# Long rows, a later sum of squares, half-K products and an early split in a two-layer decoder trunk

## The chip, the core and the metric

The kernel runs on one core of a Trainium2 chip. The core has five engines that run their own instruction streams in order: TensorE (PE for its matmuls, PEld for its weight loads), VectorE (DVE), ScalarE (ACT), GpSimd (POOL) and SyncE (SP, which here only issues DMAs). The metric is the time of one execution on the device in microseconds, the median over several runs.

## The reference

The program computes two layers of a decoder over 256 tokens plus 16 learned meta tokens put in front (272 columns in all), with a model width of 2048.

```
layer 0:  h += gla(rmsnorm(h))            # gated linear attention, 4 heads
          h += relu(rmsnorm(h) W_up)^2 W_down          # width 8192
shared:   k, v = rmsnorm(h) W_kv ; rotary on k
layer 1:  h += swa(rmsnorm(h) W_q, k, v)  # window 128, sinks, 32 query and 4 key heads
          h += relu(rmsnorm(h) W_up)^2 W_down
out = rmsnorm(h), the meta tokens dropped
```

The end of the linear attention is what the change touches most. Per head of 512 value columns:

```
o = o * rsqrt(mean(o*o) + eps) * norm_out
o = o * silu(gate)            # gate is part of xn @ w_in
h = h + o @ w_out
```

Everything is float32, and the result has to hold to nearly that precision.

## The kernel before, in words

Activations lie transposed: 128 channels of the model on the partitions, tokens along the free dimension. `h` is 16 such tiles (KT = 16) of 272 tokens. TensorE multiplies in the faster float32r format, so every operand is split in two: a high part, which is the value rounded by a cast, and a low part, the value less the high part. A product is made of three passes per k (128 rows of K): high by high, high by low, low by high.

**Weights.** `fetch` (line 79) brings half a weight tile, 128x1024 float32, by a DMA that SP issues. `split_weight` (line 86) makes its high part on ACT (line 89) and its low part on DVE (line 91); three buffers hold each. `product` (line 122) makes one output tile of 128 columns: 8 k with the first half of the weights, 8 k with the second, all into one PSUM bank of the pool `acc`, which has four. For 256 tokens `passes` (line 105) joins the two passes of the high weights in one matmul of 512 columns (lines 114 and 115), else it issues three (lines 118 to 120).

**Activations.** The class `Split` (line 98) holds both parts of an activation tile. In memory the order is (a, s, j): token 2j + a, part s, so a tile is four rows: even high, even low, odd high, odd low. The views `hi`, `lo` and `both` that the matmuls read walk through tokens in order, so they alternate between an even row and an odd row. Five places make such splits, each with one instruction on ACT for the high part and one on DVE for the low part: `split_x` (lines 161 and 162) for the inputs of each projection, the gate stage (lines 700 and 701), the MLP's hidden tiles (lines 730 and 731), and attention's output `O` (lines 899 and 900, and 932 and 933). Their producers write through the same views.

**Gate stage** (lines 668 to 702). For each head g, `mix(g)` makes four output tiles on TensorE (lines 674 to 676), copies them to `OT` on ACT, squares them on ACT and adds the squares on POOL. `so.rstd` then splits the sum (lines 188 and 189), adds over partitions by two matmuls with ones (lines 190 and 191), and derives the reciprocal root by ACT and DVE (lines 197 to 204). Four multiplications scale `OT` (line 681). After that come the head's four gate tiles: a product with 16 k (line 688), a scaling (690), a clamp on POOL (692), three ACT functions (693 to 695), two multiplications on DVE (696 and 697), and the split to `y`.

**First output projection.** `residual` (line 146) makes the 16 output tiles one after the other, each over all 16 `y`, adds each to `h` (line 151) and calls `finish`, which splits the new `h` for the MLP and adds up its squares.

**Shared K/V and layer 1's queries** (lines 788 to 806). Four K/V products run side by side in four banks, first all four with the first half of K, then all with the second. During the second half, the query inputs `xq` are split from `h`. Sixteen buffers of the tag `x` serve both the K/V input `xk` and `xq`, so an `xq` tile waits until the `xk` tile whose slot it takes has been multiplied. Eight of them are split in the loop, two after each product of the second half; the other eight follow behind the loop. A rotary step (`rope`, lines 766 to 776) on K stands between them: its DMAs go through POOL's queue and DVE waits for them at line 775.

**Order.** A planner puts the instructions in order: it simulates the engines with a cost model and takes, for each engine, what is ready, by the order of the source. In the attention stage TensorE's order is written out by hand (line 942), ACT's and DVE's is the planner's. On the chip every engine runs its list in order, and an instruction that waits holds up all behind it on that engine. `tc.issue_after(ins)` adds an edge of order only: what the block issues on the engine of `ins` comes behind `ins`; the other engines are left alone.

Of the kernel before, what the change touches and what calls it, by code (L numbers as in the profile page):

```python
# [19 lines left out]
P = 128  # L20
D = 2048
KT = D // P
HK = KT // 2
NM = 16
SEQ = 256
# [39 lines left out]
def trunk(ctx: ExitStack, tc: tile.TileContext, a: dict, out: bass.AP):  # L65
# [28 lines left out]
    def pairs_of(t):  # L94

        return t.rearrange("p (j a) -> p j a", a=2)

    class Split:


        def __init__(self, tile_, n):
            self.n, self.both = n, tile_[:, :2 * n].rearrange("p (a s j) -> p s j a", a=2, s=2)
            self.hi, self.lo = self.both[:, 0], self.both[:, 1]

    def passes(ps, hi, lo, xs, first, last, m=P, apart=True):
# [3 lines left out]
        for k, x in enumerate(xs):  # L109
            wh, wl = hi[:, k * m:(k + 1) * m], lo[:, k * m:(k + 1) * m]  # L110
            begin, end = first and k == 0, last and k == len(xs) - 1
            if wide:
                both = ps[:, :2 * n].rearrange("p (s j a) -> p s j a", s=2, a=2)
                nc.tensor.matmul(both, wh, x.both, start=begin, stop=False)  # L114
                nc.tensor.matmul(both[:, 1], wl, x.hi, start=False, stop=end)  # L115
            else:
                out = pairs_of(ps[:, :n])
                nc.tensor.matmul(out, wh, x.hi, start=begin, stop=False)  # L118
                nc.tensor.matmul(out, wh, x.lo, start=False, stop=False)  # L119
                nc.tensor.matmul(out, wl, x.hi, start=False, stop=end)  # L120

# [23 lines left out]

    def residual(src_w, ys, cols, finish, rounds=1, between=None):

        for r in range(rounds):
            for m in range(KT):
                for term in product(src_w[m], ys, halves=(0, 1) if rounds == 1 else (r,), apart=between is None or r > 0):  # L150
# [6 lines left out]

    def split_x(src, scale_col):
        x = Split(xp.tile([P, 2 * L], F32R, tag="x", name="x"), src.shape[-1])
        src = pairs_of(src)  # L160
        nc.scalar.activation(x.hi, src, AF.Copy, scale=scale_col)
        nc.vector.scalar_tensor_tensor(x.lo, src, scale_col, x.hi.bitcast(F32), ALU.mult, ALU.subtract)  # L162
        return x
# [59 lines left out]
    with ExitStack() as gla:  # L223
# [444 lines left out]
        def mix(g):  # L668
            so = Square()
            OT[g] = yp.tile([P, 4, L], F32, tag="OT", bufs=2, name="OT")  # L670
            for m in range(4):
# [6 lines left out]
                so.add(OT[g][:, m], square=nc.scalar.square)  # L678
            ro = so.rstd(512, "rso", bufs=2, split=True)
            for m in range(4):  # L680
                nc.vector.tensor_mul(OT[g][:, m], OT[g][:, m], ro)

        ys = []
        for m in range(KT):
            g, mm = divmod(m, 4)
            if mm == 0:
                mix(g)
            ps, = product(a["w_in"][32 + m], xs)
# [6 lines left out]
            nc.scalar.activation(sg, sg, AF.Exp, scale=-1.0)  # L695
            nc.vector.tensor_mul(gt, gt, sg)
            nc.vector.scalar_tensor_tensor(gt, OT[g][:, mm], no[:, mm:mm + 1], gt, ALU.mult, ALU.mult)
            y = Split(yp.tile([P, 2 * L], F32R, tag="y", bufs=KT, name="y"), L)
            gt = pairs_of(gt)
            nc.scalar.copy(y.hi, gt)  # L700
            nc.vector.tensor_sub(y.lo, gt, y.hi.bitcast(F32))
            ys.append(y)

        xs, sq = [], Square()
# [6 lines left out]

        residual(a["w_out_a"], ys, slice(0, L), next_norm(1))

    def mlp(layer, xs, sq, cols, finish):
        n = cols.stop - cols.start
        rs = sq.rstd(D, "rs", split=True)
        with tc.tile_pool(name="hid", bufs=KT) as hp, tc.tile_pool(name="wp2", bufs=1) as wp2:
            for b in range(NB):
                hs = []
                for m in range(KT):  # L720
# [7 lines left out]
                    y = Split(hp.tile([P, 2 * L], F32R, tag="hid", name="hid"), n)  # L728
                    u2 = pairs_of(u2)
                    nc.scalar.copy(y.hi, u2)  # L730
                    nc.vector.tensor_sub(y.lo, u2, y.hi.bitcast(F32))
                    hs.append(y)
# [19 lines left out]
    with ExitStack() as swa:  # L752
# [11 lines left out]
        m1, m2, m3 = ld("m1", [P, P]), ld("m2", [P, SEQ]), ld("m3", [P, L])  # L764

        def rope(dst, src, cols):

# [20 lines left out]
        kv = [acc.tile([P, 512], F32, tag="acc", name="ps") for _ in range(4)]  # L788
        xq, vts = [], []
        for i in range(2):  # L790
            for m in range(4):
                hi, lo = split_weight(fetch(a["w_kv"][m][i]))
                passes(kv[m], hi, lo, xk[i * HK:(i + 1) * HK], i == 0, i == 1)
                if i == 0:
                    continue
                xq += [split_x(h[k][:, X], qgains[:, k:k + 1]) for k in range(2 * m, 2 * m + 2)]
# [20 lines left out]

        O = ap.tile([P, KT, 2, 2, SEQ // 2], F32R, name="O")

        def attended(part, ms, tokens):  # L820

            return O[:, ms, :, part, tokens.start // 2:tokens.stop // 2].rearrange("p m a j -> p m j a")
        N1, N3 = P - NM, NM
# [26 lines left out]
        class Step:  # L850
# [39 lines left out]
            def values(self):  # L890
# [6 lines left out]
                oh, ol = (attended(part, slice(m0, m0 + 2), slice(0, N2)) for part in range(2))  # L897
                pv = pv.rearrange("p i (j a) -> p i j a", a=2)
                nc.scalar.copy(oh, pv)
# [24 lines left out]
            def last_values(self):  # L924
# [4 lines left out]
                ms = slice(self.pair * GRP, (self.pair + 1) * GRP)  # L929
                src = ps[:, :P].rearrange("p (i j a) -> p i j a", i=GRP, a=2)  # L930
                oh, ol = (attended(part, ms, slice(N2, SEQ)) for part in range(2))
# [142 lines left out]
```

## Time and profile before

| | |
|---|---|
| median of 3 runs | 2062.76 us (2061.18 to 2065.05) |
| the profiled execution | 2060.31 us |
| its span, first to last instruction | 2058.6 us |
| mean granted TensorE clock | 0.997 |
| PE busy, PEld busy | 2030.5 us, 1951.3 us |
| DVE, ACT, POOL busy | 1404.8, 1130.7, 202.3 us |
| read from HBM | 376.82 MB, 184 GB/s over the span |

Times in the profile count from the first instruction. `L91` is line 91 of the kernel. A group's row has the engine, the operation, the tiles written and read, the number of instructions, and durations in nanoseconds as least, median and greatest, or the sum of busy time and a mean. A row of waits has who waited for whom, the total in microseconds, how often, and the longest. Matmuls are pipelined and their ends are modelled, so the distance between two starts says more than a duration.

### The profile page before, as it was taken

To read this page: it belongs to the slowest core of one execution; us is meant where nothing else is said; L and a number is where in the kernel's file an instruction comes from. 1 tells how busy PE (TensorE), PEld (TensorE's weight loads), DVE (VectorE), ACT (ScalarE), POOL (GpSimd) and SP (SyncE) were. 2 spreads that over 40 slices of the span, in tenths; PEclk is the share of its full clock that TensorE was granted. 3 is DMA by queue.
4 is the path that set the end of the run, shared out by engine and by line. 5 is a ranking of instruction groups with operands and counts; after the bars stand their busy time and mean duration, and the time that the engine had idled before them with its cause. 6 is when DMAs were issued, how large, how long until landed. Compare 5 with 4: busy or idle time off the path is not lost. (4 is left out here: it accounts for less than half of the span.)

```text
span 2058.6 us, 39099 instructions
## 1 busy us (share of the span) xinstructions
PE 2030.5 (99%) x15978; PEld 1951.3 (95%) x15978; DVE 1404.8 (68%) x1999; ACT 1130.7 (55%) x1729; POOL 202.3 (10%) x209
## 2 busy tenths in 40 slices
PE   9999999999999999999999999999999999999997
PEld 9999999999999999999999988999999999999997
DVE  7799677766556556655667777697666666666776
ACT  7565665455345435534554578756546545644653
POOL 0000233300000000000024111060000000000032
PEclk9999999999999999999999999999999999999999
DMA  7644445565655555555554654466666666666662
GB/s 242 194 160 142 150 144 180 189 230 190 192 188 191 189 192 187 192 188 193 186 190 154 203 161 141 135 229 211 203 199 203 200 201 202 201 200 203 200 200 103
DMA packets 109124, 383.85 MB, mean 186 GB/s; under 512 B 13328, under 2 KB 15888, under 8 KB 108944
## 3 DMA queue, kind: packets, MB, share of 16 engines
q1 hardware_dynamic: 106640, 378.29, 56.9%
q0 software_dynamic: 1152, 2.38, 0.4%
q8 instruction: 125, 2.05, 0.4%
q10 hardware_dynamic: 1152, 0.68, 0.1%
q14 instruction: 55, 0.45, 0.1%
HBM read 376.82 MB, written 2.10 MB: 184 GB/s over the span
## 5 line engine op out<-in xcount | busy, mean ns | idle before, releaser
L91 DVE TENSOR_TENSOR lo<-raw,hi 128x1024 fp32r<-128x1024 f32 x707 | 872.4, 1235 | 468.8 <-ACT hi L89 460.8
L89 ACT CAST hi<-raw 128x1024 fp32r<-128x1024 f32 x707 | 740.4, 1048 | 782.4 <-PE ps L119 435.8
L119 PE MATMUL ps<-x,hi 128*128 128x272 f32 (+1 forms) x2032 | 567.4, 279 | 2.3 <-DVE x L162 2.3
L118 PE MATMUL ps<-x,hi 128*128 128x272 f32 (+1 forms) x2032 | 568.6, 280 | 0.0
L120 PE MATMUL ps<-x,lo 128*128 128x272 f32 (+1 forms) x2032 | 567.6, 280 | 0.3 <-DVE lo L91 0.3
L119 PEld LDWEIGHTS ps<-x,hi 128*128 128x128 f32 x2032 | 385.5, 190 | 2.9 <-DVE x L162 2.7
L118 PEld LDWEIGHTS ps<-x,hi 128*128 128x128 f32 x2032 | 385.5, 190 | 2.6 <-issue 2.1
L120 PEld LDWEIGHTS ps<-x,lo 128*128 128x128 f32 x2032 | 385.3, 190 | 1.1 <-DVE lo L91 0.6
L114 PE MATMUL ps<-x,hi 128*128 128x512 f32 x1024 | 335.9, 382 | 0.0
L114 PE MATMUL ps<-hid,hi 128*128 128x512 f32 x1008 | 330.1, 382 | 0.0
L118 PE MATMUL ps<-hid,hi 128*128 128x272 f32 (+1 forms) x1040 | 290.1, 279 | 0.0
L119 PE MATMUL ps<-hid,hi 128*128 128x272 f32 (+1 forms) x1040 | 290.1, 279 | 0.0
L120 PE MATMUL ps<-hid,lo 128*128 128x272 f32 (+1 forms) x1040 | 290.1, 279 | 0.0
L115 PE MATMUL ps<-x,lo 128*128 128x256 f32 x1024 | 279.2, 273 | 0.0
L115 PE MATMUL ps<-hid,lo 128*128 128x256 f32 x1008 | 274.1, 273 | 0.0
L114 PEld LDWEIGHTS ps<-x,hi 128*128 128x128 f32 x1024 | 193.5, 189 | 27.0 <-DVE x L162 0.2
L114 PEld LDWEIGHTS ps<-hid,hi 128*128 128x128 f32 x1008 | 190.2, 189 | 26.4
L115 PEld LDWEIGHTS ps<-x,lo 128*128 128x128 f32 x1024 | 196.6, 192 | 0.3 <-DVE lo L91 0.3
L118 PEld LDWEIGHTS ps<-hid,hi 128*128 128x128 f32 x1040 | 196.6, 189 | 0.0
L119 PEld LDWEIGHTS ps<-hid,hi 128*128 128x128 f32 x1040 | 196.6, 189 | 0.0
L120 PEld LDWEIGHTS ps<-hid,lo 128*128 128x128 f32 x1040 | 196.6, 189 | 0.0
L115 PEld LDWEIGHTS ps<-hid,lo 128*128 128x128 f32 x1008 | 193.5, 192 | 0.2
(259 smaller groups left out, 2214.0 us busy)
## 6 DMA issues: line engine op xcount, KB each, us to landing
raw<-in_w_up SPq DMA_DIRECT2D x256, 512.0 KB, 4.2
raw<-in_w_down SPq DMA_DIRECT2D x256, 512.0 KB, 4.2
raw<-in_w_in SPq DMA_DIRECT2D x91, 512.0 KB, 3.4
raw<-in_w_out_a SPq DMA_DIRECT2D x32, 512.0 KB, 4.0
raw<-in_w_q SPq DMA_DIRECT2D x32, 512.0 KB, 3.6
raw<-in_w_out_b SPq DMA_DIRECT2D x32, 512.0 KB, 3.4
raw<-in_w_kv SPq DMA_DIRECT2D x8, 512.0 KB, 3.5
sw<-qt POOLq DMA_DIRECT2D x32, 64.0 KB, 4.3
```

What stands on the lines that cost most here:

```text
L89: nc.scalar.copy(hi, raw)
L91: nc.vector.tensor_sub(lo, raw, hi.bitcast(F32))
L114: nc.tensor.matmul(both, wh, x.both, start=begin, stop=False)
L115: nc.tensor.matmul(both[:, 1], wl, x.hi, start=False, stop=end)
L118: nc.tensor.matmul(out, wh, x.hi, start=begin, stop=False)
L119: nc.tensor.matmul(out, wh, x.lo, start=False, stop=False)
L120: nc.tensor.matmul(out, wl, x.hi, start=False, stop=end)
```

## The change

Four edits.

1. *Rows.* `Split` gets two more views, `hi_runs` and `lo_runs`, that walk through all even tokens and then all odd ones. The producers (the five places above) write through them and read their source at a step of two tokens. What lies in memory, and what the matmuls read, is as before. For `O` the same is done in `attended` and in the views of its PSUM source.
2. *Squares.* `mix` no longer ends with the sum. A new `mixed(g, so)` holds it, with its matmuls ordered behind the newest gate matmul (`newest[0]`). The loop over heads makes `mix`, the first two gate products with their activation functions (`gate_product`), then `mixed`, then the gating and split of these two tiles (`gated`), and then the other two tiles whole.
3. *Halves of K.* `residual` gets `begin`; the first output projection passes 3. The first three output tiles run side by side in three banks: first half of K for all three, then the second half.
4. *Early split.* `split_x` can write into a given place. Eight of the query inputs (k from 8 to 15) are split during the first half of the K/V products, into the tiles of `O`, which attention fills only later; `O` is declared earlier for it.

```diff
+    def runs_of(t):
+        return t.rearrange("p (j a) -> p a j", a=2)
 class Split:
+            runs = tile_[:, :2 * n].rearrange("p (a s j) -> p s a j", a=2, s=2)
+            self.hi_runs, self.lo_runs = runs[:, 0], runs[:, 1]
+    newest = [None]
 def passes(...)
-                nc.tensor.matmul(out, wl, x.hi, start=False, stop=end)
+                newest[0] = nc.tensor.matmul(out, wl, x.hi, start=False, stop=end)
-    def residual(src_w, ys, cols, finish, rounds=1, between=None):
+    def residual(src_w, ys, cols, finish, rounds=1, between=None, begin=0):
+            if begin:
+                banks = [acc.tile([P, 512], F32, tag="acc", name="ps") for _ in range(begin)]
+                for i in range(2):
+                    for m, ps in enumerate(banks):
+                        hi, lo = split_weight(fetch(src_w[m][i]))
+                        passes(ps, hi, lo, ys[i * HK:(i + 1) * HK], i == 0, i == 1)
+                        if i == 1:
+                            nc.vector.tensor_add(h[m][:, cols], h[m][:, cols], ps[:, :ys[0].n])
+                            finish(m)
-            for m in range(KT):
+            for m in range(begin, KT):
-    def split_x(src, scale_col):
-        x = Split(xp.tile([P, 2 * L], F32R, tag="x", name="x"), src.shape[-1])
-        src = pairs_of(src)
-        nc.scalar.activation(x.hi, src, AF.Copy, scale=scale_col)
-        nc.vector.scalar_tensor_tensor(x.lo, src, scale_col, x.hi.bitcast(F32), ALU.mult, ALU.subtract)
+    def split_x(src, scale_col, room=None):
+        x = Split(xp.tile([P, 2 * L], F32R, tag="x", name="x") if room is None else room, src.shape[-1])
+        src = runs_of(src)
+        nc.scalar.activation(x.hi_runs, src, AF.Copy, scale=scale_col)
+        nc.vector.scalar_tensor_tensor(x.lo_runs, src, scale_col, x.hi_runs.bitcast(F32), ALU.mult, ALU.subtract)
...
-            ro = so.rstd(512, "rso", bufs=2, split=True)
+            return so
+        def mixed(g, so):
+            with tc.issue_after(newest[0].ins):
+                ro = so.rstd(512, "rso", bufs=2, split=True)
             for m in range(4):
                 nc.vector.tensor_mul(OT[g][:, m], OT[g][:, m], ro)
...
+        for g in range(GH):
+            so = mix(g)
+            waiting = [gate_product(4 * g + m) for m in range(2)]
+            mixed(g, so)
+            for m, gt in enumerate(waiting):
+                gated(4 * g + m, gt)
+            for m in range(2, 4):
+                gated(4 * g + m, gate_product(4 * g + m))
-        residual(a["w_out_a"], ys, slice(0, L), next_norm(1))
+        residual(a["w_out_a"], ys, slice(0, L), next_norm(1), begin=3)
...
                 if i == 0:
+                    late_xq += [split_x(h[k][:, X], qgains[:, k:k + 1], O[:, k].rearrange("p a s j -> p (a s j)")) for k in range(HK + 2 * m, HK + 2 * m + 2)]
                     continue
...
-        xq += [split_x(h[k][:, X], qgains[:, k:k + 1]) for k in range(HK, KT)]
+        xq += late_xq
```

The splits of the gate stage, the MLP and attention change in the same way as `split_x`: `runs_of` in place of `pairs_of` for the source, and the `_runs` views for the target.

More of the change, by code (lines that the diff above doesn't have):

```diff
@@ L114, in passes @@
                 nc.tensor.matmul(both, wh, x.both, start=begin, stop=False)
-                nc.tensor.matmul(both[:, 1], wl, x.hi, start=False, stop=end)
+                newest[0] = nc.tensor.matmul(both[:, 1], wl, x.hi, start=False, stop=end)
             else:
@@ L683, in trunk, with gate_product @@
         ys = []
[L684 to L687, printed above, removed]
+        def gate_product(m):
             ps, = product(a["w_in"][32 + m], xs)
@@ L696, in trunk, with gated @@
             nc.vector.tensor_mul(gt, gt, sg)
+            return gt
+        def gated(m, gt):
+            g, mm = divmod(m, 4)
             nc.vector.scalar_tensor_tensor(gt, OT[g][:, mm], no[:, mm:mm + 1], gt, ALU.mult, ALU.mult)
             y = Split(yp.tile([P, 2 * L], F32R, tag="y", bufs=KT, name="y"), L)
-            gt = pairs_of(gt)
-            nc.scalar.copy(y.hi, gt)
-            nc.vector.tensor_sub(y.lo, gt, y.hi.bitcast(F32))
+            gt = runs_of(gt)
+            nc.scalar.copy(y.hi_runs, gt)
+            nc.vector.tensor_sub(y.lo_runs, gt, y.hi_runs.bitcast(F32))
             ys.append(y)
+        for g in range(GH):
[6 more added lines that the diff above has]
+                gated(4 * g + m, gate_product(4 * g + m))
         xs, sq = [], Square()
@@ L728, in mlp @@
                     y = Split(hp.tile([P, 2 * L], F32R, tag="hid", name="hid"), n)
-                    u2 = pairs_of(u2)
-                    nc.scalar.copy(y.hi, u2)
-                    nc.vector.tensor_sub(y.lo, u2, y.hi.bitcast(F32))
+                    u2 = runs_of(u2)
+                    nc.scalar.copy(y.hi_runs, u2)
+                    nc.vector.tensor_sub(y.lo_runs, u2, y.hi_runs.bitcast(F32))
                     hs.append(y)
@@ L764, in trunk @@
         m1, m2, m3 = ld("m1", [P, P]), ld("m2", [P, SEQ]), ld("m3", [P, L])
+        O = ap.tile([P, KT, 2, 2, SEQ // 2], F32R, name="O")
         def rope(dst, src, cols):
@@ L788, in trunk @@
         kv = [acc.tile([P, 512], F32, tag="acc", name="ps") for _ in range(4)]
-        xq, vts = [], []
+        xq, late_xq, vts = [], [], []
         for i in range(2):
@@ L815, in token_major @@
                 nc.scalar.copy(VT[i][:n, g], pt[:n, i * P:(i + 1) * P])
-        O = ap.tile([P, KT, 2, 2, SEQ // 2], F32R, name="O")
         def attended(part, ms, tokens):
-            return O[:, ms, :, part, tokens.start // 2:tokens.stop // 2].rearrange("p m a j -> p m j a")
+            return O[:, ms, :, part, tokens.start // 2:tokens.stop // 2]
         N1, N3 = P - NM, NM
@@ L897, in values @@
                 oh, ol = (attended(part, slice(m0, m0 + 2), slice(0, N2)) for part in range(2))
-                pv = pv.rearrange("p i (j a) -> p i j a", a=2)
+                pv = pv.rearrange("p i (j a) -> p i a j", a=2)
                 nc.scalar.copy(oh, pv)
@@ L929, in last_values @@
                 ms = slice(self.pair * GRP, (self.pair + 1) * GRP)
-                src = ps[:, :P].rearrange("p (i j a) -> p i j a", i=GRP, a=2)
+                src = ps[:, :P].rearrange("p (i j a) -> p i a j", i=GRP, a=2)
                 oh, ol = (attended(part, ms, slice(N2, SEQ)) for part in range(2))
```

## The prediction

> **What bounds the kernel now.** I read first the page's first part, then the busy time of each engine by stage (I cut the span where the source changes what it does), then who the weight loads waited for, then the timeline around those waits.
>
> ```profile
> span 2058.6 us, 39099 instructions
> PE 2030.5 (99%) x15978; PEld 1951.3 (95%) x15978; DVE 1404.8 (68%) x1999; ACT 1130.7 (55%) x1729; POOL 202.3 (10%) x209
> ```
>
> By stage; the columns are length of the stretch, then PE, PEld, DVE, ACT, POOL busy:
>
> ```profile
> 216.00:325.00 109.00, 104.98 (x858) 103.34 (x858) 78.52 (x129) 71.52 (x145) 33.52 (x27) 0.98 0.45 146
> 325.00:420.00 95.00, 93.17 (x798) 92.42 (x797) 69.24 (x74) 49.92 (x59) 38.33 (x33) 1.00 0.60 192
> 420.00:1128.00 708.00, 708.00 (x6115) 708.00 (x6113) 421.90 (x467) 343.16 (x401) 32.36 (x29) 1.00 0.58 190
> 1128.00:1160.00 32.00, 29.65 (x254) 29.16 (x253) 26.74 (x42) 21.54 (x33) 4.49 (x6) 1.00 0.60 182
> 1160.00:1332.00 172.00, 167.36 (x1470) 154.16 (x1469) 115.84 (x292) 131.24 (x354) 21.54 (x40) 0.99 0.50 157
> 1332.00:1375.00 43.00, 43.00 (x265) 39.62 (x265) 40.97 (x60) 25.80 (x30) 31.57 (x27) 1.00 0.58 184
> 1375.00:2045.00 670.00, 670.00 (x4105) 616.12 (x4104) 456.03 (x584) 355.00 (x466) 35.71 (x34) 1.00 0.62 198
> ```
>
> TensorE is the limit. In the two MLPs (420 to 1128 and 1375 to 2045) it is never idle, and the matmuls there stay the same in number, size and operands. So 1378 us of the span can't move, whatever becomes cheaper on ACT and DVE. What can move is TensorE's idle time in four stages: gate (4.02), first output projection (1.83), shared K/V (2.35), attention (4.64), together 12.8 us. This is the ceiling, but for the first 20 us. Whom the weight loads waited for (total us, times, longest) says which of it the change touches; the weight load is the better witness, since a matmul's modelled end covers a part of each gap:
>
> ```profile
> PEld ps_ssq L190 <- ACT sqh L188: 4.1, 2, 2.1
> PEld ps L119 <- DVE x L162: 2.7, 2, 1.5
> PEld ps_pv L896 <- ACT PT L887: 2.6, 3, 1.9
> PEld s L874 <- DVE O L933: 1.8, 1, 1.8
> PEld pt L885 <- DVE mx L829: 1.4, 2, 1.0
> ```
> ```profile
> PEld ps L119 <- DVE y L701: 1.1, 1, 1.1
> PEld ps L118 <- ACT y L700: 0.8, 1, 0.8
> ```
>
> The first is the sum of squares in the gate stage, the second the query input after K/V, the next three lie in attention, the last two are the last gate tiles.
>
> **1. Long rows.** Before, a split (L161/L162, L700/L701, L730/L731, L899/L900, L932/L933) reads its source straight and writes two far rows in turn. After, it reads every second element and writes each row in one piece. Same count of instructions. Durations in ns, min/median/max:
>
> ```profile
> L730 ACT CAST hid<-u x128: 663/675/697, 429.4 to 1965.9; 128x272 fp32r<-128x272 f32 x64, 128x256 fp32r<-128x256 f32 x64
> L188 ACT CAST sqh<-ssq x7: 408/420/420, 227.0 to 1380.9; 128x272 fp32r<-128x272 f32 x6, 128x256 fp32r<-128x256 f32 x1
> L731 DVE TENSOR_TENSOR hid<-u,hid x128: 608/626/660, 430.7 to 1966.7; 128x272 fp32r<-128x272 f32 x64, 128x256 fp32r<-128x256 f32 x64
> L189 DVE TENSOR_TENSOR sql<-ssq,sqh x7: 411/436/443, 227.4 to 1381.8; 128x272 fp32r<-128x272 f32 x6, 128x256 fp32r<-128x256 f32 x1
> L535 DVE TENSOR_TENSOR W<-E,K x12: 678/691/705, 114.0 to 188.5; 128x512 f32<-128x512 f32 x12
> ```
>
> L188 and L189 are the same cast and subtraction, straight on both sides: 0.25 us less on ACT, 0.19 on DVE. That stepped reading is free I take from L535: its twelve runs go through the six levels, from straight runs to every second element on both sides, and lie within 678 to 705 ns. So a split costs about 0.42 + 0.44 after. Bounds: those, or the old time. For the 128 MLP splits this saves 128 x (0.25 + 0.19) = 56 us of engine time and nothing of the end: the cover is the fully busy TensorE of the MLP rows above, where DVE has 286 and 214 us to spare. It counts only where a split ends a wait, below. In the first microseconds it does: the first two x splits feed the first matmuls directly. The first, at 3.4 us, is
>
> ```profile
> 3.40 0.76 ACT L161 ACTIVATE x<-h,gains 128x272 fp32r<-128x272 f32 x1 [0.58 <-DMA gains<-in_gains]
> ```
>
> and loses some 0.3 on ACT. DMA and weight splits set most of the pace there: **-0.3** (0 to -0.7).
>
> **2. Squares summed two gate tiles later.** The two PE matmuls of the sum (L190, L191) are ordered behind gate tile 4g+1 instead of standing wherever the planner put them; only their place moves, and no DMA. For the last head the mix's last matmul started at 300.4, and then:
>
> ```profile
> L676 PE MATMUL ps_o<-AT,V x32: 271/274/275, 220.6 to 300.4; 128*128 128x128 f32 x32
> ```
> ```profile
> 308.39 0.41 ACT L188 CAST sqh<-ssq 128x272 fp32r<-128x272 f32 x1
> ```
> ```profile
> 308.86 0.39 PE L190 MATMUL ps_ssq<-sqh,ones_r 128*128 128x272 f32 x1 [1.74 <-ACT sqh L188]
> ```
> ```profile
> L681 DVE TENSOR_TENSOR OT<-OT,rstd x16: 428/434/648, 235.7 to 319.9; 128x272 f32<-128x272 f32 x16
> ```
>
> TensorE, in order, stood 1.7 to 1.9 us for sqh. One k of a product takes 0.35 us (L118 at 324.96 and again at 325.31, below), so a gate tile takes 16 x 0.35 = 5.6 and two end at about 300.4 + 0.3 + 11.2 = 311.9. sqh is done at 308.8, its low part some 1.3 later: both are there. The two waits of 4.1 go: **-4.0** (0 to -4.1). Late next: OT's scaling and the first two tiles' gating. OT's last scaling was only at 319.9 (L681), 8 us after that, so its date hardly changes.
>
> **3. First three output products by halves of K.**
>
> ```profile
> 324.96 0.28 PE L118 MATMUL ps<-y,hi 128*128 128x272 f32 x1
> ```
> ```profile
> 325.31 0.28 PE L118 MATMUL ps<-y,hi 128*128 128x272 f32 x1
> ```
> ```profile
> 335.58 0.66 ACT L700 CAST y<-gt 128x272 fp32r<-128x272 f32 x1 [1.85 <-DVE gt L697]
> ```
> ```profile
> 336.27 0.64 DVE L701 TENSOR_TENSOR y<-gt,y 128x272 fp32r<-128x272 f32 x1 [0.72 <-ACT y L700]
> ```
> ```profile
> L690 DVE TENSOR_TENSOR gt<-ps,rstd x16: 434/435/445, 225.3 to 329.2; 128x272 f32<-128x272 f32 x16
> ```
>
> Same 144 passes, same six weight halves (and their DMAs) in another order, three accumulator banks of four held (the tiles before have left theirs: the last gate read, L690, is at 329.2, before the third bank's turn at 330.6). From 324.96, three first halves take 3 x 8 x 0.35 = 8.4 us, then y[15] is wanted after 7 more k, at 335.8. With the row writes it comes whole at 335.58 + 0.41 + 0.06 + 0.44 = 336.5. Of 1.1 + 0.8 = 1.9 some 0.5 stays: **-1.4** (0 to -1.9).
>
> **4. Half of layer 1's input split early.** Eight of the sixteen xq tiles no longer wait for a slot of x (all sixteen are held by xk until its last pass) but go into O during the first K/V half.
>
> ```profile
> 1155.78 0.72 DVE L775 TENSOR_TENSOR sw<-sw,sin 128x544 f32<-128x544 f32 x1 [1.79 <-DMA sw<-kt]
> 1156.42 1.16 DVE L162 SCALAR_TENSOR_TENSOR x<-h,qgains,x 128x256 fp32r<-128x256 f32 x2
> 1157.41 1.22 DVE L91 TENSOR_TENSOR lo<-raw,hi 128x1024 fp32r<-128x1024 f32 x1
> 1158.55 0.66 DVE L162 SCALAR_TENSOR_TENSOR x<-h,qgains,x 128x256 fp32r<-128x256 f32 x1
> ```
> ```profile
> L162 DVE SCALAR_TENSOR_TENSOR x<-h,qgains,x 128x256 fp32r<-128x256 f32 x16 | 9.4, 754 | 0.0
> ```
>
> The last three x stood behind a rotary step (L775) for which DVE waited 1.79 us on a DMA, and TensorE lost 2.7 on them. Eight splits moved forward are 8 x 0.5 = 4 us of DVE; thirteen of sixteen were done before the L775 wait, so all of them fit with eight moved. What is late next is the weight split L91 behind the same L775 (without the x it ends at about 1157.6); the next product wants it near 1158. **-2.4** (-0.5 to -2.7). O is not written by attention until the last query has read x: no new wait there.
>
> **5. Attention.** The O splits stand in front of the masks and score banks whose lateness stopped TensorE.
>
> ```profile
> L900 DVE TENSOR_TENSOR O<-ps_pv,O x8: 984/1026/1061, 1216.0 to 1327.2; 128x480 fp32r<-128x480 f32 x8
> ```
>
> A DVE operation of two inputs and 512 elements takes 0.69 (L535). So L900, of 480, goes from 1.03 to about 0.67, once in each of three waits (longest 1.9, 1.8 and 1.0): 3 x 0.36 = **-1.1**. No row here reads PSUM at a step of two, so the price is bounded from both sides: 0.36 cheaper, or 0.36 dearer (+1.1); I take the near row.
>
> [...]
>
> **Sum.** -0.3 - 4.0 - 1.4 - 2.4 - 1.1 = -9.2. The profiled execution took 2060.31 us (span 2058.6 and 1.7 around it), so 2051.1 for one like it. The median of the runs, 2062.76, lies 2.45 above it, and I predict that median: 2062.76 - 9.2 = **2053.6**. I take no change for anything within 0.2% (4.1 us), about what a measurement of this kernel can tell.
>
> **The rivals.**
>
> (a) *More closes.* All idle time of the four stages goes: 2062.8 - 12.8 = 2050.0. For it: attention's waits are short and the splits are faster everywhere. Against: three of them end on exponentials and mask steps that stay.
>
> (b) *Waits move.* The planner orders ACT and DVE anew. If the sum's cast again stands behind a weight split, one of its two waits stays (-2.0); if the L91 behind L775 stops the next product, K/V gives 1.2; the rest of the gate's end and attention gives 0.8. -4.0: 2058.8. For it: what was late was the cast L188, whose place on ACT is the planner's. Against: it may now come 3.1 us later (311.9 against 308.8).
>
> (c) *Slower: the gating bunches.* Place: gate tiles 4g+2 and 4g+3, where all that waited for the sum now falls due.
>
> ```profile
> L697 DVE SCALAR_TENSOR_TENSOR gt<-OT,norm_out,gt x16: 490/502/945, 237.4 to 335.0; 128x272 f32<-128x272 f32 x16
> ```
>
> DVE then has, in two tiles (11.2 us): four weight splits at 1.23 (L91), four OT scalings at 0.43, five operations of the sum at 0.44, the two tiles' own L690 and L696 at 0.43, and four L697 with their low part, 0.94 each: 4.9 + 1.7 + 2.2 + 1.7 + 3.8 = 14.3, that is 3.1 too many. It decides once the weights' lead is under 3.1 us; then each of four heads stops TensorE for 3.1, and the last y, behind the last bunch, keep their wait: 12.4 - 9.2 + 1.4 = +4.6: 2067.4. For it: DVE is in order and a low weight part stands behind what was planned first. Against: weights are three halves ahead (two of 2.8 us besides the one in use), and DVE has 30 of the stage's 109 us free.
>
> (d) *The rows aren't shorter.* Reading every second element costs what writing two rows cost, and more: between 1332 and 1375 DVE is busy 40.97 of 43, so 14 x splits there, each dearer by as much as L162 takes above (0.75), make 10.5 - 2.0 = +8.5. With K/V and gate as forecast but the gate's end at -0.9: 8.5 - 4.0 - 0.9 - 2.4 = +1.2: 2064.0. L535 speaks against it.
>
> **How the numbers follow.** Forecast 0.60, (a) 0.10, (b) 0.17, (c) 0.09, (d) 0.04. Faster by over 0.2% is below 2058.6: the forecast, (a), and of (b), which sits on the line, 0.05: 0.75. Within 0.2%: the rest of (b) and (d): 0.16. Slower: (c), 0.09. The range goes from below (a) to above (b): 2049 to 2060.5, which also holds the terms' bounds (all at their best -10.5 without moving anything else; without attention and the start -7.8, with the weak end of K/V too -5.9, with attention's dear end as well -4.8); outside stay (c), (d) and a little of (a) and (b).
>
> **What would show it.** The splits' rows: L730's line near 0.42 instead of 0.675 and L731's near 0.44 (step 1). No wait of the ssq matmul for sqh (2). The weight loads of the y passes wait 0.5 or less, and three products are open at once (3). No wait for x at the first query, and eight L162 of the query input before the second K/V half (4). L900 near 0.67 and attention's idle at 3.5 (5). TensorE still busy throughout both MLPs; any idle time there would show that the plan's new order, which I priced only where it meets a wait, went elsewhere, and the prediction would be wrong. So it would with new low-part waits (L91) between 216 and 325.

## The result, and the profile after

| | before | after |
|---|---|---|
| median, runs on one chip | 2063.91 us (2061.18 to 2065.08) | 2049.25 us (2047.53 to 2049.9) |
| ratio, 95% interval | | 0.993 (0.9912 to 0.9947) |
| profiled execution, its span | 2060.31, 2058.6 us | 2047.53, 2045.8 us |

The kernel became 0.7% faster. The profiled execution lost 12.8 us and the median on this chip 14.7, where 9.2 were forecast. 2049.25 lies just inside the lower end of the range (2049.0).

The first part of the page, after:

```profile
span 2045.8 us, 39103 instructions
PE 2023.8 (99%) x15978; PEld 1946.6 (95%) x15978; DVE 1364.8 (67%) x1999; ACT 1088.0 (53%) x1729; POOL 201.7 (10%) x209
```

DVE has 40.0 us less to do and ACT 42.7, with as many instructions as before. Where that came out is told by the stages. The same view as before, of the changed kernel (length, then PE, PEld, DVE, ACT, POOL busy, granted clock, DMA share, GB/s); as everything is earlier, the stretches begin and end earlier too:

```profile
216.00:320.00 104.00, 103.11 (x858) 101.56 (x857) 71.68 (x120) 69.16 (x145) 33.74 (x27) 1.00 0.48 152
415.00:1123.00 708.00, 708.00 (x6115) 708.00 (x6114) 406.20 (x466) 324.60 (x400) 32.35 (x29) 1.00 0.57 190
1123.00:1152.00 29.00, 29.00 (x254) 28.88 (x253) 23.62 (x40) 19.72 (x33) 4.49 (x6) 1.00 0.64 195
1152.00:1320.00 168.00, 165.57 (x1471) 153.64 (x1470) 113.66 (x293) 127.26 (x354) 20.46 (x40) 1.00 0.50 161
```

The MLP is as full as it was. K/V has no idle TensorE left, attention has 2.43 us instead of 4.64. The clock column now says 1.00 in all these rows; before it said 0.98 in the gate stage and 0.99 in attention, and the prediction quoted these rows and read past that column.

The lines of the splits (busy time in us, mean in ns):

```profile
L762 ACT CAST hid<-u 128x272 fp32r<-128x272 f32 x64 | 29.0, 453 | 2.0
L763 DVE TENSOR_TENSOR hid<-u,hid 128x272 fp32r<-128x272 f32 x64 | 27.7, 434 | 0.0
L724 DVE TENSOR_TENSOR y<-gt,y 128x272 fp32r<-128x272 f32 x16 | 6.6, 431 | 0.0
L932 ACT CAST O<-ps_pv 128x480 fp32r<-128x480 f32 x8 | 4.5, 558 | 1.4 <-PE ps_pv L929 1.4
L933 DVE TENSOR_TENSOR O<-ps_pv,O 128x480 fp32r<-128x480 f32 x8 | 5.2, 651 | 0.0
```

L762 and L763 are the old L730 and L731, L932 and L933 the old L899 and L900. A split of 272 columns takes 0.45 + 0.43; one of 480, read from PSUM at a step of two, 0.56 + 0.65 instead of 1.03 + 1.03. The 64 splits of `x` that also scale (the old L161 and L162) gained less: in the median 0.56 + 0.88 instead of 0.78 + 1.05.

Whom the weight loads waited for, after. First the gate stage and the start of the projection (216 to 345), then attention (1150 to 1330):

```profile
PEld ps L128 <- DVE lo L91: 1.5, 3, 0.8
PEld ps L126 <- ACT hi L89: 1.1, 1, 1.1
PEld ps L127 <- DVE y L724: 0.8, 1, 0.8
```
```profile
PEld s L907 <- DVE O L966: 1.4, 1, 1.4
PEld ps_pv L961 <- ACT PT L953: 1.2, 2, 1.0
PEld s L939 <- POOL qs L898: 0.8, 1, 0.8
PEld pt L918 <- DVE mx L862: 0.4, 1, 0.4
PEld ps_pv L929 <- ACT PT L920: 0.2, 1, 0.2
```

The sum of squares stops nobody any more, and neither does `x` after K/V. In their place weight parts are late in the gate stage and at the start of the projection, by 2.6 together (1.1 before).

Between fixed matmuls of both traces the time went so (us; the start, counted from TensorE's first instruction at 1.11, to the first mix; from there to the last product of `w_out_a`; from there over the first MLP to its last product; to the first score; to the last value product; to the first product of layer 1's `hid`; the rest):

| | start | gate and projection | MLP 0 | K/V, queries | attention | to MLP 1 | rest |
|---|---|---|---|---|---|---|---|
| before | 218.84 | 196.71 | 711.93 | 55.87 | 142.16 | 132.12 | 599.85 |
| after | 218.99 | 191.17 | 711.93 | 52.98 | 138.10 | 131.67 | 599.86 |
| difference | +0.15 | -5.54 | 0 | -2.89 | -4.06 | -0.45 | 0 |
| forecast | -0.3 | -5.4 | 0 | -2.4 | -1.1 | 0 | 0 |

So the sizes agree in three stages, and attention gave nearly four times its term. But two agreeing sums needn't have the same parts, and the experiments show that they haven't.

### The profile page after: what moved, and what is told of

Read it like the earlier page. It is cut to its first block, busy times and chain, and to the rows that moved or that the text cites. A ratio compares the mean times of both kernels' runs of the same rounds, so it can differ in the third digit from the quotient of the medians.

```text
span 2045.8 us, 39103 instructions
## 1 busy us (share of the span) xinstructions
PE 2023.8 (99%) x15978; PEld 1946.6 (95%) x15978; DVE 1364.8 (67%) x1999; ACT 1088.0 (53%) x1729; POOL 201.7 (10%) x209
## 4 chain that ended last, share of the span: by engine, by line
PE 86%; DVE 5%; ACT 4%; issue 2%; POOL 1%; DMA 1%; SPq 0%; DVEq 0%; ACTq 0%; POOLq 0%
PE ps L122 23%; PE ps L128 16%; PE ps L126 16%; PE ps L127 16%; PE ps L123 12%; DVE lo L91 1%; POOL sg L711 1%; ACT hi L89 1%; ACT pr L874 1%; ACT pr L879 1%; DVE pr L862 1%; DMA sw<-qt 1%; PE ps L305 1%; DMA raw<-in_w_in 0%; ACT PT L920 0%
## 5 line engine op out<-in xcount | busy, mean ns | idle before, releaser
L91 DVE TENSOR_TENSOR lo<-raw,hi 128x1024 fp32r<-128x1024 f32 x707 | 871.9, 1234 | 487.4 <-ACT hi L89 479.3
L128 PE MATMUL ps<-x,lo 128*128 128x272 f32 (+1 forms) x1904 | 531.8, 280 | 1.0 <-DVE lo L91 0.9
L126 PE MATMUL ps<-x,hi 128*128 128x272 f32 (+1 forms) x1904 | 531.6, 279 | 0.0
L127 PE MATMUL ps<-x,hi 128*128 128x272 f32 (+1 forms) x1904 | 531.1, 279 | 0.0
L128 PEld LDWEIGHTS ps<-x,lo 128*128 128x128 f32 x1904 | 359.9, 189 | 2.3 <-DVE lo L91 1.8
L126 PEld LDWEIGHTS ps<-x,hi 128*128 128x128 f32 x1904 | 360.2, 189 | 0.6 <-issue 0.4
L127 PEld LDWEIGHTS ps<-x,hi 128*128 128x128 f32 x1904 | 360.2, 189 | 0.1
L122 PEld LDWEIGHTS ps<-x,hi 128*128 128x128 f32 x1024 | 193.5, 189 | 27.0
L123 PEld LDWEIGHTS ps<-x,lo 128*128 128x128 f32 x1024 | 196.6, 192 | 0.0
```

Source lines behind the costliest of these rows:

```text
L91: nc.vector.tensor_sub(lo, raw, hi.bitcast(F32))
L123: newest[0] = nc.tensor.matmul(both[:, 1], wl, x.hi, start=False, stop=end)
L128: newest[0] = nc.tensor.matmul(out, wl, x.hi, start=False, stop=end)
```

## The experiments

Each edit is made to the changed kernel unless it says otherwise. Kernels that stand together in a list ran on one chip beside the kernel before. First, each part of the change by itself or taken away.

**Rows undone.** All five places write two rows in turn again ("far rows" from here on, against the "long rows" of edit 1); edits 2, 3 and 4 stay.

```diff
-        src = runs_of(src)
-        nc.scalar.activation(x.hi_runs, src, AF.Copy, scale=scale_col)
+        src = pairs_of(src)
+        nc.scalar.activation(x.hi, src, AF.Copy, scale=scale_col)
...
```

> All row writes are undone (the five kinds of split read straight and write two rows in turn, as before); the later squares, the half-K products and the early split stay. Theory A (attention's 4.1 us, of which I had priced 1.1, come from the shorter splits of O): attention from the first score matmul to the last output product takes as long as before, the gate and K/V stages keep nearly all of their 5.4 and 2.9; the span is about 2051.5. Theory B (they come from another order of ACT and DVE that the early split and the other moves bring with them): attention keeps its 4, the span is about 2047.5. Both MLPs stay fully busy either way.

**Rows alone.** Edits 2, 3 and 4 undone.

```diff
-            with tc.issue_after(newest[0].ins):
-                ro = so.rstd(512, "rso", bufs=2, split=True)
+            ro = so.rstd(512, "rso", bufs=2, split=True)
...
-        residual(a["w_out_a"], ys, slice(0, L), next_norm(1), begin=3)
+        residual(a["w_out_a"], ys, slice(0, L), next_norm(1))
...
-        xq += late_xq
+        xq += [split_x(h[k][:, X], qgains[:, k:k + 1]) for k in range(HK, KT)]
```

> Only the row writes are made; squares, output products and the query input's split stay as before. Theory A: attention gains 4, the rest about 0.5 to 1, the span is about 2053.5. Theory B: attention gains 1.1 or less, the span is about 2057. Engine time falls by about 40 us on DVE and on ACT in both, and the MLPs gain nothing.

**Rows of O undone.** Only attention's output is written in two rows in turn.

```diff
-                pv = pv.rearrange("p i (j a) -> p i a j", a=2)
+                pv = pv.rearrange("p i (j a) -> p i j a", a=2)
...
```

> The changed kernel with the rows of O alone undone (the four instructions after attention's value products read PSUM straight and write two rows in turn). Theory A: attention loses 3 to 4 us, the span is about 2049.5. Theory B: it loses 1 or less, the span is about 2046.5.

**Early split undone.**

```diff
-                    late_xq += [split_x(h[k][:, X], qgains[:, k:k + 1], O[:, k].rearrange("p a s j -> p (a s j)")) for k in range(HK + 2 * m, HK + 2 * m + 2)]
...
-        xq += late_xq
+        xq += [split_x(h[k][:, X], qgains[:, k:k + 1]) for k in range(HK, KT)]
```

> The changed kernel with the early split alone undone (eight query inputs are split behind the K/V loop again, with row writes). My term for it was 2.4. Theory A: K/V loses 1.5 to 2.4, attention keeps its gain, the span is about 2048. Theory B: attention loses its 3 to 4 as well, the span is about 2051.5.

Measured: the medians, the ratio to the kernel before on that chip (2063.36), and the stages of each trace, in which the first MLP and the rest stay as they are:

| | median | ratio (95%) | gate, proj. | K/V | attention | to MLP 1 |
|---|---|---|---|---|---|---|
| rows undone | 2049.91 | 0.9941 (0.9925 to 0.9958) | 187.15 | 54.16 | 141.81 | 132.57 |
| rows alone | 2050.71 | 0.9945 (0.993 to 0.996) | 190.94 | 54.21 | 139.84 | 131.67 |
| rows of O undone | 2052.22 | 0.9952 (0.9937 to 0.9967) | 191.19 | 53.00 | 141.93 | 131.67 |
| early split undone | 2050.32 | 0.9942 (0.9927 to 0.9957) | 191.15 | 54.56 | 140.25 | 131.67 |

What follows. The parts stand in for each other and don't add up: the rows alone bring the span from 2058.6 to 2048.9, all the rest without them to 2047.2, both together to 2045.8. The early split is worth 1.58 in K/V (54.56 against 52.98); rows alone still lose time to an `x` there. Attention loses 3.71 with all rows undone and 3.83 with those of `O` alone undone, which is theory A; but it also loses 2.15 without the early split, which leaves its code alone, so neither theory holds by itself. Long rows of the second MLP's inputs and hidden tiles give the 0.45 on the way to MLP 1: it is there in every kernel that has them and in none that hasn't. And one thing was not foreseen at all: with far rows (rows undone) the gate stage takes 187.15, four microseconds less than after, and no weight load waits there for anything.

The order of instructions is the same in both, on every engine. The line that differs most is the clamp on POOL (`tensor_scalar_max`, L711, before L692; durations, first and last start) of before, after and rows undone:

```profile
L692 POOL TENSOR_SCALAR sg<-gt x16: 887/1789/2634, 226.9 to 329.7; 128x272 f32<-128x272 f32 x16
```
```profile
L711 POOL TENSOR_SCALAR sg<-gt x16: 887/1788/3919, 223.9 to 325.3; 128x272 f32<-128x272 f32 x16
```
```profile
L711 POOL TENSOR_SCALAR sg<-gt x16: 884/915/1020, 223.5 to 320.4; 128x272 f32<-128x272 f32 x16
```

The same instruction takes 0.89 us or up to 3.9. The timeline of the changed kernel around its last clamp (start, duration; POOL and DVE):

```profile
325.05 0.43 DVE L724 TENSOR_TENSOR y<-gt,y 128x272 fp32r<-128x272 f32 x1
325.29 3.92 POOL L711 TENSOR_SCALAR sg<-gt 128x272 f32<-128x272 f32 x1 [6.07 <-ACT y L723]
325.41 1.20 DVE L91 TENSOR_TENSOR lo<-raw,hi 128x1024 fp32r<-128x1024 f32 x1
326.55 0.78 DVE L724 TENSOR_TENSOR y<-gt,y 128x272 fp32r<-128x272 f32 x2
327.25 1.21 DVE L91 TENSOR_TENSOR lo<-raw,hi 128x1024 fp32r<-128x1024 f32 x1
```

DVE's instructions, each with two inputs in SBUF, follow one another without a gap until 328.46, and the clamp, which takes 0.89 at least, ends at 329.21, three quarters of a microsecond behind the last of them: most of it ran only when DVE had paused. So it takes 3.92 beside such a run. The first clamp, at 223.87, takes 0.89; DVE starts its next two-input instruction only at 224.21.

The next four kernels tell the clamp from the rows and from edits 2 and 3.

**Rows of y undone.** Only the gate stage's splits write two rows in turn.

```diff
-            gt = runs_of(gt)
-            nc.scalar.copy(y.hi_runs, gt)
-            nc.vector.tensor_sub(y.lo_runs, gt, y.hi_runs.bitcast(F32))
+            gt = pairs_of(gt)
+            nc.scalar.copy(y.hi, gt)
+            nc.vector.tensor_sub(y.lo, gt, y.hi.bitcast(F32))
```

> The changed kernel with the rows of the gate tiles y alone undone. The run with all rows undone took 187.15 us from the first mix to the last y product, 4.0 less than the changed kernel with the same TensorE order. Theory L (POOL's clamp of the gate is held up by the DVE instruction with two SBUF operands that happens to start beside it, and everything behind it, ACT's functions, the gating and the weight splits, comes late; the y splits' length decides what starts beside it): the stage takes about 187.5, the span is about 2042. Theory X (the 4.0 come from something else that the other rows changed): it stays near 191, the span is about 2046.5 or more, since the y splits are longer.

**Clamp on DVE.** Rows as after.

```diff
-            nc.gpsimd.tensor_scalar_max(sg, gt, -80.0)
+            nc.vector.tensor_scalar_max(sg, gt, -80.0)
```

> The changed kernel with the gate's clamp (the larger of gate and -80) moved from POOL to DVE: 16 instructions of some 0.3 to 0.45 us more on DVE, none of 0.9 to 3.9 on POOL. [...] Theory X: DVE only gets 6 us more in a stage where it sets the weights' dates; the stage stays at 191 or grows by 1 to 3, the span is 2046 to 2049.

**Later sum undone** (edit 2).

```diff
-            with tc.issue_after(newest[0].ins):
-                ro = so.rstd(512, "rso", bufs=2, split=True)
+            ro = so.rstd(512, "rso", bufs=2, split=True)
...
-            waiting = [gate_product(4 * g + m) for m in range(2)]
             mixed(g, so)
-            for m, gt in enumerate(waiting):
-                gated(4 * g + m, gt)
-            for m in range(2, 4):
+            for m in range(4):
                 gated(4 * g + m, gate_product(4 * g + m))
```

> The changed kernel with the later sum of squares alone undone (the sum stands right behind the mix, and the gating follows each gate tile). My term: 4.0. In the run with row writes alone, which has the early sum too, only one of its two waits was left (1.5 us). So by my term the span is about 2050; if most of the sum's waits go with the shorter splits anyway, first mix to last y takes 191.2 to 193 and the span is 2046 to 2048.

**Halves of K undone** (edit 3).

```diff
-        residual(a["w_out_a"], ys, slice(0, L), next_norm(1), begin=3)
+        residual(a["w_out_a"], ys, slice(0, L), next_norm(1))
```

> The changed kernel with the half-K products alone undone (the first output products run one after the other again). My term: 1.4. By it the span is about 2047.3. If the changed kernel's waits for weights at the first half-K product (1.1 and 0.8 us) are the price of this edit, it is 2044 to 2046.

Measured, beside a kernel before of 2061.31:

| | median | ratio (95%) | gate, proj. | K/V | attention |
|---|---|---|---|---|---|
| rows of y undone | 2044.97 | 0.9915 (0.9901 to 0.993) | 187.16 | 53.12 | 139.05 |
| clamp on DVE | 2045.45 | 0.992 (0.9906 to 0.9935) | 187.16 | 53.01 | 141.74 |
| later sum undone | 2048.0 | 0.9931 (0.9914 to 0.9947) | 189.90 | 53.07 | 139.46 |
| halves of K undone | 2050.06 | 0.994 (0.9925 to 0.9955) | 191.92 | 52.99 | 139.57 |

What follows. Two edits with nothing in common but the clamp bring the gate stage to the same 187.16 and leave no wait of a weight load in it. That the figure is the same says only that nothing waits; and moving the clamp gives ACT and DVE another order in this stage too. Rows of `y` undone is the clean one: every engine has the order of after. On DVE the clamp takes 0.30. Who waited for it on ACT (after, then rows of `y` undone) shows how it gets to TensorE:

```profile
ACT sg L712 <- POOL sg L711: 25.5, 15, 3.0
```
```profile
ACT sg L712 <- POOL sg L711: 4.8, 11, 0.6
```

ACT is in order; while it stands for a clamp, the high parts of weights and of `y` stand behind. The stretch around the third head's last gate tile shows the difference at its start. After, and then with rows of `y` undone:

```profile
297.94 0.43 DVE L724 TENSOR_TENSOR y<-gt,y 128x272 fp32r<-128x272 f32 x1
298.17 2.78 POOL L711 TENSOR_SCALAR sg<-gt 128x272 f32<-128x272 f32 x1 [6.07 <-ACT OT L694]
298.29 1.22 DVE L91 TENSOR_TENSOR lo<-raw,hi 128x1024 fp32r<-128x1024 f32 x1
```
```profile
294.86 0.63 DVE L724 TENSOR_TENSOR y<-gt,y 128x272 fp32r<-128x272 f32 x1
295.10 1.01 POOL L711 TENSOR_SCALAR sg<-gt 128x272 f32<-128x272 f32 x1 [6.07 <-ACT OT L694]
295.34 1.38 DVE L91 TENSOR_TENSOR lo<-raw,hi 128x1024 fp32r<-128x1024 f32 x1
```

TensorE, DVE and ACT have the same order of instructions in these two kernels, from the first to the last. With far rows the clamp gets in, and it is L91 that takes 1.38 instead of 1.22; with long rows L91 comes first and the clamp waits. Why the slower write lets the clamp in isn't shown by a row. Nor is it a rule: the kernel before and rows alone also have the same order on every engine, and there the long rows go with shorter waits of ACT for the clamp (before, then rows alone), and the stage falls from 196.71 to 190.94. In both pairs the stage falls with ACT's waits for the clamp. Here the shorter splits may have a part of their own; in the pair of after and rows of `y` undone they got longer, and the stage fell all the same.

```profile
ACT sg L693 <- POOL sg L692: 23.0, 13, 2.6
```
```profile
ACT sg L711 <- POOL sg L710: 14.9, 10, 2.6
```

Undoing edits 2 and 3 gives other waits in the same stretch. Later sum undone, and then halves of K undone:

```profile
PEld ps_ssq L207 <- ACT sqh L205: 1.5, 1, 1.5
```
```profile
PEld ps L126 <- ACT y L723: 1.2, 1, 1.2
```

Without the later sum its cast is waited for again, but the stage is 1.27 shorter (189.90 against 191.17). Without the halves of K it is 0.75 longer.

The last four: after and rows of `y` undone once more beside each other, the clamp's move on the kernel before, and a try at the best of all.

**After again**, no edit.

> The changed kernel once more, for a second profile and beside the next runs. Theory H (TensorE's clock falls to half speed for one stretch of 3.41 us after some of its waits, at a price of 1.7 us each, and whether a wait is caught depends on the moment; the first profile of before has two such stretches, the changed kernel's first profile none): the gate stage takes 191.2 or 192.9, attention 138 to 140 or 1.7 more, the other stages the same to 0.1. Rival (the stages differ between profiles only because of the kernels' order): all stages repeat within 0.2 us.

**Rows of y undone again**, the edit shown above.

> The changed kernel with the rows of y undone, once more, beside the changed kernel itself. By the first run it is 4.0 us less in the gate stage: 0.998 of the changed kernel's time. Theory H gives attention 138 to 140.5 or 1.7 more.

**Clamp alone.** The kernel before, with one word changed.

```diff
-            nc.gpsimd.tensor_scalar_max(sg, gt, -80.0)
+            nc.vector.tensor_scalar_max(sg, gt, -80.0)
```

> The kernel of before with only the gate's clamp moved from POOL to DVE. Theory L (POOL's clamp, 1.79 us there in the median, held up by DVE's two-operand instructions, makes the gating late) says that part of the 9.6 us which the gate stage loses against its undisturbed 187.15 goes without any of the change's edits: with POOL's time on the squares' additions left, 2 to 6 of them; the span is 2052.5 to 2056.5. If the sum's place alone made the waits, it stays at 2058 to 2059.

**Best.** Rows of `y` undone, the last value products one slot later, and the query copy that the scores waited 0.8 for on DVE.

```diff
-                    nc.gpsimd.tensor_copy(self.qs[:, 2 * self.j * N3:2 * (self.j + 1) * N3].rearrange("p (i q) -> p i q", i=2), self.QR[:, :, N2:])
+                    nc.vector.tensor_copy(self.qs[:, 2 * self.j * N3:2 * (self.j + 1) * N3].rearrange("p (i q) -> p i q", i=2), self.QR[:, :, N2:])
...
-                        slots[2].append(old.last_values)
+                        slots[3].append(old.last_values)
```

> The changed kernel with y's rows undone, the last value products of a key pair one slot later, and the copy of the last queries on DVE instead of POOL. In the changed kernel's attention the weight loads waited 1.4 us for O's low part (a score bank held by these value products), 1.2 for their transposed probabilities and 0.8 for the copy on POOL. If these waits can be taken one by one, attention falls by 2 to 3 and the span is about 2040; if the next thing on ACT is late at the same place, it stays at 2042 to 2043.

Measured, beside a kernel before of 2061.58:

| | median | ratio (95%) | gate, proj. | K/V | attention |
|---|---|---|---|---|---|
| after again | 2049.61 | 0.9942 (0.9928 to 0.9955) | 191.19 | 52.98 | 137.91 |
| rows of y undone again | 2044.52 | 0.9919 (0.9906 to 0.9933) | 187.15 | 53.00 | 139.17 |
| clamp alone | 2054.05 | 0.9967 (0.9954 to 0.9979) | 187.17 | 58.93 | 143.05 |
| best | 2049.47 | 0.994 (0.9927 to 0.9952) | 187.16 | 53.32 | 143.92 |

What follows. The traces repeat: each stage of the two kernels that ran twice is within 0.2 us of its first trace. That is the rival's forecast, and theory H's as well where no half clock shows; what decides stands under the clock, below. Rows of `y` undone beats both kernels: all its runs (2043.55 to 2046.93) lie below all of after (2047.37 to 2050.64). The clamp alone, on the kernel before, takes 9.54 us off the gate stage and projection, with neither the later sum nor the halves of K: first mix and last product of `w_out_a` in the kernel before, then in clamp alone:

```profile
L674 PE MATMUL ps_o<-AM,VM x16: 288/370/381, 219.9 to 299.6; 80*128 80x272 f32 x16
L120 PE MATMUL ps<-y,lo x256: 279/279/383, 325.2 to 416.6; 128*128 128x272 f32 x128
```
```profile
L674 PE MATMUL ps_o<-AM,VM x16: 288/369/381, 220.6 to 295.6; 80*128 80x272 f32 x16
L120 PE MATMUL ps<-y,lo x256: 279/279/279, 319.2 to 407.8; 128*128 128x272 f32 x128
```

So the waits that edits 2 and 3 were priced by, the sum's cast included, are gone without these edits once the clamp is moved. How much of the 9.54 is the clamp and how much the order isn't separated: the one word also changes ACT's and DVE's order in this stage, and TensorE's in the third and fourth head. The forecast had been 2 to 6. The time fell by less, 4.8 in the span and 7.5 in the median: K/V became 3.06 longer, with 3.1 us of waits for `x` (2.7 before) and half clock behind them, and attention 0.89. Best was a miss, with a span of 2048.4 where 2040 or at most 2043 was expected: the scores no longer wait for `O`, but the last products then do, for 4.2 us,

```profile
PEld ps L126 <- ACT O L965: 4.2, 1, 4.2
```

because one slot later for the values is one slot later for `O`. Its two moves in attention weren't tried apart.

**The clock.** The kernel before, around the two waits that its clock column pointed at (columns as above; the last but two is the granted clock):

```profile
277.00:279.00 2.00, 0.63 (x5) 0.63 (x5) 1.27 (x3) 1.57 (x3) 0.10 (x1) 1.00 0.00 0
279.00:281.00 2.00, 2.00 (x12) 1.93 (x12) 1.74 (x4) 1.97 (x4) 0.04 (x1) 0.66 0.00 0
281.00:283.00 2.00, 2.00 (x11) 2.00 (x10) 1.86 (x4) 0.28 (x2) 1.75 (x1) 0.50 0.73 219
283.00:285.00 2.00, 2.00 (x19) 2.00 (x18) 1.14 (x3) 1.94 (x4) 0.00 (x0) 0.98 0.83 246
...
1228.00:1230.00 2.00, 1.88 (x10) 0.85 (x12) 0.47 (x1) 2.00 (x5) 0.00 (x0) 0.64 0.65 231
1230.00:1232.00 2.00, 2.00 (x16) 1.69 (x14) 2.00 (x3) 1.62 (x2) 0.00 (x0) 0.51 0.19 41
```

Behind a wait the clock is halved for (0.34 + 0.50 + 0.02) x 2 / 0.5 = 3.4 us, and TensorE, which the busy column still shows as full, does 11 or 12 matmuls in 2 us instead of 19. That is 3.4 / 2 = 1.7 us of TensorE's work, here twice; the execution can lose less by it, where a later wait becomes shorter. In neither trace of after does it happen in these stages. Which wait sets it off hangs on more than its length. Clamp on DVE, and then halves of K undone, around the same wait in attention:

```profile
1252.00:1254.00 2.00, 1.12 (x12) 0.71 (x10) 1.89 (x3) 0.69 (x3) 0.00 (x0) 1.00 0.80 262
1254.00:1256.00 2.00, 1.84 (x9) 1.35 (x10) 1.97 (x13) 0.79 (x5) 0.00 (x0) 0.76 0.76 258
1256.00:1258.00 2.00, 2.00 (x11) 2.00 (x11) 1.49 (x9) 2.00 (x11) 0.00 (x0) 0.50 0.01 4
```
```profile
1256.00:1258.00 2.00, 0.96 (x12) 0.56 (x10) 2.00 (x4) 0.51 (x2) 0.00 (x0) 1.00 0.78 262
1258.00:1260.00 2.00, 2.00 (x14) 1.62 (x15) 1.97 (x14) 0.95 (x5) 0.00 (x0) 1.00 0.82 262
```

About the same idle time, and the half clock behind it in the one and not in the other. By the clock column the two stretches of the kernel before begin at 279.66 and 1228.56 and last 3.413 us each; the second begins 278.0 times that length behind the first. Whether stretches can begin only at fixed times, which would explain why one wait is hit and its like isn't, is not shown by these two. The busy time of the whole 3.41 us ahead doesn't decide either: in the kernel before TensorE was busy for 1.67 of the 3.41 us from 306.97 with no half clock behind them, in clamp on DVE for 2.37 of those from 1251.64, and the half clock followed. What sets it off stays open. The half clock stands in the traces of rows undone, rows of `O` undone and clamp on DVE once in attention, in clamp alone once there and for 6.8 us in K/V (58.93, of which up to 3.4 are this), in best for 6.8. The other traces have none in these stages. Each kernel has one trace or two, but the mean granted clock was measured in every execution. Over 23 executions of the kernel before it goes from 0.994 (four, with spans of 2061.6 to 2063.9) to 0.998 (three, 2058.2 to 2058.5), so the stretches come and go in one kernel, as theory H has it. Its price doesn't hold as well: 0.004 of the clock is 16.5 us at half clock, nearly five stretches, for some 4.6 us, about 1 us each by this estimate; and the profiled execution, with two of them, took 2058.6, hardly more than the three at 0.998.

## Why the prediction was right or wrong

**The sum.** By stages, the forecast of -9.2 missed -12.8 by 3.6: attention 2.96, K/V 0.5, `x` after attention 0.45, gate 0.14, and the start 0.45 the other way. The direction held. The rival "more closes", 2050.0, came nearest in time, but not as it said, since gate and attention kept waits.

**1. Long rows: right in price, wrong in one place.** 0.42 + 0.44 were forecast, 0.45 + 0.43 measured for `hid` and `y`; the scaled splits of `x`, priced the same, take 0.56 + 0.88. Stepped reading is nearly free (0.45 + 0.43, where the straight L188 and L189 took 0.42 + 0.44), and from PSUM it didn't undo the gain: 0.56 and 0.65 for 480 elements where 1.03 stood. The MLPs hid all of it, as forecast: 711.93 us in every trace. The -0.3 at the start didn't come (+0.15, where the repeats differ by up to 0.14). What the step lacked is that a cheaper instruction changes who gets in beside it: with edits 2 and 3 in place the long rows of `y` alone cost 4.0 us of the gate stage.

**2. Squares later: the wait went, its term didn't stand.** No weight load waits for sqh, as forecast. But the term took the wait for the edit's to give, and what the edits are worth hangs on the rows: with far rows edits 2 and 3 take 9.56 off the stage (196.71 to 187.15), with long rows they add 0.23 (190.94 to 191.17). Between kernels of one order the stage falls with ACT's waits for the clamp, which the prediction never priced; its line is not among those it shows. Without edit 2 the changed kernel waits 1.5 for sqh and is yet shorter in this stage by 1.27. The forecast's own sign of failure, new low-part waits between 216 and 325, showed in part (L91, 1.5 in three, where 0.6 in one stood before). Rival (c), gating that bunches, had this place but another mechanism and three times the price.

**3. Halves of K: about half.** -1.4 was forecast; undoing it costs 0.75, with the `y` wait at 0.8 instead of 0.5. With the clamp on DVE it has nothing to do: the stage takes 187.17 without edits 2 and 3 and 187.16 with them.

For 2 and 3 together -5.4 was forecast and -5.54 measured. That they agree is an accident: 3.7 of the measured is what the waits of weight loads lost, 3.4 after against 7.1 before (4.1, 1.1 and 0.8 as quoted, and 1.1 in this row of the kernel before, which the prediction left out). The other 1.8 fits the half clock behind a wait of the kernel before, which the prediction had no term for.

```profile
PEld ps L120 <- DVE lo L91: 1.1, 2, 0.6
```

**4. Early split: right.** -2.4 forecast, -2.89 measured, no `x` wait left. Undone, 1.58 comes back rather than 2.4, since the long rows by then do part of it.

**5. Attention: mis-sized, -4.06 for -1.1.** Most of it is seen in the weight loads' waits: for `O` 1.8 became 1.4, for the maxima 1.4 became 0.4, for the PT of the first value products 2.6 became 0.2, and a wait of 0.8 for the query copy is new: 0.4 + 1.0 + 2.4 - 0.8 = 3.0. The other 1.1 has the size of the half clock at 1228, which went. Rows of `O` undone has the waits so:

```profile
PEld s L907 <- DVE O L966: 1.8, 1, 1.8
PEld pt L918 <- DVE mx L862: 1.3, 2, 1.0
PEld s L939 <- POOL qs L898: 1.1, 1, 1.1
```

By these waits the rows of `O` are worth 0.4 + 0.9 + 0.3 = 1.6, where 1.1 was forecast: the step's mechanism, and somewhat larger; the rest of this kernel's 3.83 holds a half-clock stretch and a longer wait for PT (0.8). The wait for PT is another matter. After has 0.2, halves of K undone, whose code differs from after only in a stage 750 us earlier, has

```profile
PEld ps_pv L929 <- ACT PT L920: 1.9, 2, 1.6
```

TensorE's order in this stage is the same in both. The wait repeats when a kernel runs again, so it isn't noise; what sets it stays open.

**The ceiling was wrong.** 12.8 us of idle TensorE was called the most that could move. The clamp's move, with the order that came with it, took 9.5 from stages where 5.85 us were idle: a matmul's modelled end covers part of a gap (before, the matmuls waited 3.7 us for sqh, their weight loads 4.1), and half-clock time counts as busy (before, 2.00 of the 2.00 us from 281 on, at a clock of 0.50). Rows of `y` undone has a span 15.8 below before.

## What to carry to other kernels

Before pricing the removal of a wait, follow the late instruction back to the first one that took longer than its own least duration: here POOL's clamp, 0.89 at least and 1.79 in the median, stood ahead of waits on four different lines, and all four went when it moved. An elementwise instruction on POOL beside a DVE that seldom pauses is worth trying on DVE; here it took 0.30 us there. Read the granted-clock column with the idle time: a stage at 0.98 hides time that the busy column calls work, and parts of a change that remove the same wait don't add up.

## What was not expected of the hardware

- A POOL instruction of 0.89 us was held for as long as 3.92 by DVE's two-input instructions; in two kernels with the same order it got in beside a DVE instruction that wrote far rows (1.01) and not beside one that wrote long rows (2.78).
- Waits of about 2 us were enough, in some traces and not in others, for 3.4 us of half clock; two such stretches of one trace began 278.0 times 3.413 us apart.
- Reading every second fp32 cost ACT 0.03 us in 272 columns and DVE nothing that can be seen, from SBUF (0.45 and 0.43, against 0.42 and 0.44 straight). From PSUM no straight read stands beside it; the stepped ones took 0.56 and 0.65 for 480.
